# A two-layer decoder trunk: second norm row, weight low parts, forget gates, output projection and last norm rearranged together

## The chip, the cores and the metric

The kernel runs on one core of a Trainium2 chip. The metric is the time of one execution on the device, in microseconds (us), as the median of several runs. The engines are named as the profile names them: PE (TensorE, the matrix engine), DVE (VectorE), ACT (ScalarE), POOL (GpSimd) and SP (SyncE, which here only issues DMAs). Each engine works through its own list of instructions in order. An instruction whose input is not ready holds back everything behind it on that engine.

## The reference

The input is one sequence of 1024 tokens with 1024 channels, in float32. Layer 0 is a gated linear recurrence, layer 1 is forgetting attention, and a last RMSNorm follows.

```python
def lru_mixer(h, ...):
    u = h @ w_in
    xb, gate = u[..., :1536], u[..., 1536:]
    xc = causal_depthwise_conv(xb, conv_w, conv_b)
    r, i = sigmoid(block_diag(xc, wa, ba)), sigmoid(block_diag(xc, wx, bx))
    a = exp(-8.0 * r * softplus(-a_param))
    hs = associative_scan(combine, (a, sqrt(1 - a * a) * (i * xc)))
    return (hs * silu(gate)) @ w_out

def fox_mixer(h, ...):
    q, k, v, gate, f_logit = split(h @ w_in)          # 16 heads of 64
    cum = cumsum(log_sigmoid(f_logit + b_f))
    logits = q @ k.T / 8 + (cum_q - cum_k)            # causal
    o = softmax(logits) @ v
    return (o * silu(gate)) @ w_out

x = x + lru_mixer(rms_norm(x, g0), ...)
x = x + fox_mixer(rms_norm(x, g1), ...)
out = rms_norm(x, final_g)
```

## The kernel before

Every float32 product is made of three matmuls. Weights and activations are split into a high part and a low part (the rest), and `gemm_steps` (L115) multiplies high by high, weight low by high, and weight high by low, into one PSUM tile of 128x512. A weight tile is loaded (`wf`, three buffers), ACT casts its high part `wh` (`to_hi`, L85), and one engine makes the low part `wl = wf - wh` (`to_lo`, L96). That engine is `nc.gpsimd`, unless the caller names another. `wh` and `wl` have four buffers each. The sequence has two halves of 512 tokens; `c`, `h` or `half` counts them.

**Layer 0** loops over 12 blocks `n` of 128 channels: `ups` is the block's input projection, `gps` its gate's, `ops` the output projection. The first norm's factors come from `rms_row` (which calls `inv_rms`, L139): PE sums squares (`sscol`), ACT takes the root, DVE puts the inverse on the diagonal of `rs`, PE spreads it over the partitions (`rsrow`, against `onesf`), and ACT copies that back into `rs`. The norm is applied to the products afterwards: `us = ups * rs` on DVE (L271). In block 1, `ups` is two tiles, one for each half (451 and 452 in the rows below, from weights 441/442 and 447/448).

**Layer 1 begins** with `project` and `kq_units` (keys and queries of a pair of heads), then `values(0)`, which computes the values of four heads and, in 16 more columns, the forget logits `fz`. `forget(half)` transposes four `fz` tiles (`fps`), and computes the cumulated gates of that half. Constants are set on POOL and DVE on the way: `T` and `U` (rows of ones and zeros in the operands of the logits), and the causal `mask`.

**Attention** goes over 16 heads in 8 pairs. `maxima` computes blocks of logits `S`, their maxima on DVE (L673) and exponentials `p` on ACT (L678); `weigh` transposes `p` (`pt`), splits it (`ph`, `pl`) and multiplies with the values (`O`). An order string in `run` interleaves both with steps of a generator `fill`: the next pair's projections (`kq_units`, `g_units`), and after every fourth head `values(g)`, one by one without cover. At the end of a head `tr` transposes the inverse sums, two DMAs spread them over 64 partitions (`recd`, `recb`), POOL multiplies them into the gate (`scale`, L705), and `gated` multiplies the head pair's result `yo` by it on POOL (L760). Results of pairs 0 to 5 go to `y1d` in DRAM, those of the last are split where they are (`split_y`).

**From head 12 on** no more projections are left, and `fill` is the output projection: `load_y` fetches the six stored pairs of a half, `split_loaded` casts them (`yhh`, `yhl`), and `partial` multiplies them for an output block `db` and a half `c` (`ops1`). `turned(c, q)` completes quarters: it transposes the stored sum (`x1`, from `residual`) into a PSUM tile `turn`, adds the products of the last two pairs, and takes squares (ACT L867) and the weighted copy `res` (DVE L869, L872) for the last norm. Two quarters run beside head 15, two are the tail of the kernel.

The order on each engine comes from a scheduler that runs over a simulated time line. `tc.issue_after` and the order of the generators in the code bind it.

## Time and profile before

| | |
|---|---|
| median of 3 runs | 1154.62 us (1153.79 to 1159.84) |
| the profiled execution's own time | 1156.08 us |
| its span, first to last instruction | 1154.1 us |
| DVE busy | 723.0 us (63%) |
| ACT busy | 593.2 us (51%) |
| POOL busy | 230.1 us (20%) |
| low parts on POOL (L96) | 114 instructions, 166.2 us |

The span is the stretch that the trace covers; 1.98 us of the execution lie around it. Busy times are sums over the whole span. A row of a time line gives the start, the duration, the engine, the line, the operation and its tiles; what stands in square brackets is how long the engine had been idle and what it was waiting for.

### The profile page before, as it was taken

The page shows a single profiled execution, that of the slowest core. Times are in us where ns is not written, and L with a number is a line of the kernel's source. Part 1 is how long each engine was busy: PE and PEld are TensorE (multiplying, and loading weights), DVE is VectorE, ACT ScalarE, POOL GpSimd, SP SyncE. Part 2 cuts the span into 40 slices and gives each one's busy share as a digit, 9 for nine tenths or more (in the row PEclk, how much of TensorE's full clock was granted, in tenths as well). Part 3 has the DMA queues.
Part 4 walks back from the last instruction along what each step waited for, and adds up shares of the span by engine and source line. Part 5 has one row for each costly group of instructions (what it writes and reads, how often), then busy time and mean ns, then how long its engine had stood idle before and what let it go on. Part 6 is the DMA issues. An engine that isn't in the chain of part 4 may idle for free.

```text
span 1154.1 us, 15825 instructions
## 1 busy us (share of the span) xinstructions
PE 1121.8 (97%) x5713; PEld 942.8 (82%) x5713; DVE 723.0 (63%) x1222; ACT 593.2 (51%) x1081; POOL 230.1 (20%) x159
## 2 busy tenths in 40 slices
PE   9999999999999999999999999999999999979996
PEld 7788888888888887978888988889888898858874
DVE  7589766777567789566665356663666535746644
ACT  8388345355553657455555355554555534534434
POOL 1212112211121102342222122222232221011010
PEclk9999999999999999999999999999999999989999
DMA  6111111111111124353434135241352512835444
GB/s 212 51 41 51 46 56 52 41 55 41 51 55 40 56 64 157 88 134 88 120 84 107 46 88 124 79 119 45 77 129 74 129 44 67 237 104 160 130 128 182
DMA packets 63637, 105.42 MB, mean 91 GB/s; under 512 B 9444, under 2 KB 24420, under 8 KB 63560
## 3 DMA queue, kind: packets, MB, share of 16 engines
q1 hardware_dynamic: 63560, 104.42, 31.6%
q8 instruction: 45, 0.74, 0.3%
q14 instruction: 32, 0.26, 0.1%
HBM read 63.30 MB, written 15.93 MB: 69 GB/s over the span
## 4 chain that ended last, share of the span: by engine, by line
PE 86%; DVE 4%; issue 3%; DMA 3%; POOL 2%; ACT 2%; SPq 0%; POOLq 0%; ACTq 0%; DVEq 0%
PE gps L54 31%; PE ops L54 16%; PE ups L54 11%; PE vps L54 6%; PE S L54 6%; PE O L54 5%; PE pt L58 5%; PE gate L54 3%; PE turn L54 2%; DMA recb<-recd 1%; POOL sg L705 1%; POOL wl L96 1%; DMA recd<-rc 1%; DVE sq L162 1%; DVE hl L238 1%
## 5 line engine op out<-in xcount | busy, mean ns | idle before, releaser
L96 POOL TENSOR_TENSOR wl<-wf,wh 128x512 fp32r<-128x512 f32 (+1 forms) x114 | 166.2, 1463 | 664.3 <-ACT wh L85 472.2
L54 PE MATMUL gps<-hh,wh 128*128 128x512 f32 x576 | 228.9, 398 | 0.2 <-DVE qkl L565 0.2
L54 PE MATMUL gps<-hh,wl 128*128 128x512 f32 x576 | 226.7, 394 | 0.1
L54 PE MATMUL gps<-hl,wh 128*128 128x512 f32 x576 | 226.7, 393 | 0.0
L678 ACT ACTIVATE p<-S,m 128x128 f32<-128x128 f32 (+7 forms) x128 | 94.8, 741 | 141.1 <-DVE m L673 139.7
L85 ACT CAST wh<-wf 128x512 fp32r<-128x512 f32 (+2 forms) x156 | 94.4, 607 | 141.1 <-PE ops L54 41.9
L96 DVE TENSOR_TENSOR pl<-pt,ph 128x512 fp32r<-128x512 f32 (+1 forms) x198 | 98.8, 541 | 101.6 <-ACT ph L85 101.1
L54 PEld LDWEIGHTS gps<-hl,wh 128*128 128x128 f32 x576 | 108.2, 188 | 24.5
L54 PEld LDWEIGHTS gps<-hh,wl 128*128 128x128 f32 x576 | 108.7, 189 | 20.4 <-POOL wl L96 0.6
L54 PEld LDWEIGHTS gps<-hh,wh 128*128 128x128 f32 x576 | 108.5, 188 | 20.0 <-DVE qkl L565 0.4
L673 DVE CUSTOM_DVE_ANT_0 S<-S,mask 128x128 f32<-128x128 f32 (+7 forms) x128 | 97.4, 762 | 40.5 <-PE S L54 39.0
L85 ACT CAST ph<-pt 128x512 fp32r<-128x512 f32 (+1 forms) x198 | 83.0, 474 | 28.9 <-PE pt L58 23.5
L54 PE MATMUL S<-T,U 96*128 96x512 f32 (+7 forms) x384 | 92.1, 349 | 0.0
L361 DVE TENSOR_TENSOR x<-x,ops 128x512 f32<-128x512 f32 x80 | 54.1, 682 | 50.9 <-PE ops L54 50.8
L58 PE MATMUL pt<-ident,p 128*128 128x128 f32 x576 | 80.0, 275 | 0.0
L54 PEld LDWEIGHTS S<-T,U 128*128 128x128 f32 (+1 forms) x384 | 69.1, 190 | 13.2 <-ACT p L678 0.8
L54 PE MATMUL ups<-hh,wh 128*128 128x512 f32 x192 | 76.7, 400 | 2.5 <-DVE us L271 1.9
L58 PEld LDWEIGHTS pt<-ident,p 128*128 128x128 f32 x576 | 69.2, 142 | 10.7 <-issue 0.4
L54 PE MATMUL ups<-hl,wh 128*128 128x512 f32 x192 | 76.5, 398 | 0.2
L54 PE MATMUL ops<-yh,wh 128*128 128x512 f32 x192 | 76.1, 396 | 0.5 <-DVE x L453 0.5
L54 PE MATMUL vps<-wl,hh 128*128 128x256 f32 (+1 forms) x256 | 72.8, 286 | 3.7 <-POOL wl L96 3.7
L54 PE MATMUL ups<-hh,wl 128*128 128x512 f32 x192 | 76.0, 396 | 0.0
(176 smaller groups left out, 2184.3 us busy)
## 6 DMA issues: line engine op xcount, KB each, us to landing
wf<-in_w SPq DMA_DIRECT2D x100, 256.0 KB
wf<-in_wo SPq DMA_DIRECT2D x64, 128.0 KB
U<-qkh SPq DMA_DIRECT2D x64, 128.0 KB
T<-qkh SPq DMA_DIRECT2D x28, 256.0 KB
x<-in_xt SPq DMA_DIRECT2D x16, 256.0 KB
x1d<-x SPq DMA_DIRECT2D x16, 256.0 KB
wf<-in_wv SPq DMA_DIRECT2D x16, 256.0 KB
U<-qkl SPq DMA_DIRECT2D x32, 128.0 KB
```

Source lines behind the costliest of these rows:

```text
L54: pe[0] = nc.tensor.matmul(*args, **kw)
L58: pe[0] = nc.tensor.transpose(*args)
L85: nc.scalar.copy(hi, src)
L96: return eng.tensor_tensor(lo, src, f32(hi), ALU.subtract)
L162: eng.tensor_tensor(parts[0], parts[0], sq, ALU.add)
L238: nc.vector.scalar_tensor_tensor(lo, x, g_, f32(hi), ALU.mult, ALU.subtract)
L361: nc.vector.tensor_tensor(x, x, pt, ALU.add)
L673: nc.vector.tensor_tensor_reduce(S[:, :n], S[:, :n], mask[:, SEQ - n :], -1.0, -NEG, ALU.add, ALU.min, accum_out=m)
L678: seen[0] = nc.scalar.activation(p, S[:, :n], AF.Exp, bias=m, scale=-1.0, accum_out=sums[:, i : i + 1])
L705: nc.gpsimd.tensor_tensor(sg, sg, recs[hd // 2][rows, cs], ALU.mult)
```

## The change

It has eight parts, all in the order or the place of work. The arithmetic stays.

1. In block 1 of layer 0 the first half's product is issued in steps. The second four weight rows (wh 447) come after the second norm row.
2. The constants `T`, `U` and `mask` are set in the code after two steps of `values(0)`, not ahead of it.
3. `forget` becomes a generator, and its second half runs among the key and query projections.
4. `values(1)` to `values(3)` begin ahead of the last head's second run, and make low parts on DVE.
5. `kq_units` and `g_units` make low parts on DVE for pairs 1 to 7.
6. From head 12 on, the stored results are cast beside the gate projection and the first `partial`, the output blocks go two at a time, weights of the next block are split one earlier, and the last but one pair's results are split one run later.
7. The first quarter's stored sums are loaded into eight tiles of the values' pool, and the others into swapped tags.
8. In the tail, `turn` takes one-bank PSUM tiles with tag `g` or `O`, and the scaling of the first half's output becomes a side generator.

```diff
@@ layer 0
-            product(ups[0], 0, wu)
+            steps = gemm_steps(ups[0], zip(wu, raw[0]))
+            if n == 1:
+                take(steps, 2)
+                with tc.issue_after(row.ins):
+                    drain(steps)
+            drain(steps)
...
-                rms_row(sums[1], rs[:, HALF:])
+                row = rms_row(sums[1], rs[:, HALF:])[2]
@@ constants: the memsets of T and U become fixed_rows(), called below with the mask
@@ values
-                parts += split_weights(src, (2, 256 + ex), nc.scalar, nc.gpsimd)
+                parts += split_weights(src, (2, 256 + ex), nc.scalar, nc.gpsimd if ex else nc.vector)
+                if k == 2:
+                    yield
@@ kq_units, g_units
+        def low(pair):
+            return nc.vector if pair else nc.gpsimd
-                    kqw[is_k] = list(weights(w1[is_k * 8 + pair]))
+                    kqw[is_k] = list(weights(w1[is_k * 8 + pair], lo_eng=low(pair)))
-                gw[0] = list(weights(w1[16 + pair]))
+                gw[0] = list(weights(w1[16 + pair], lo_eng=low(pair)))
@@ forget
             for i in range(4):
-                transpose(pt[:HEADS, i * P : (i + 1) * P], fz[:, half * 4 + i], ident)
+                if half and i > 1:
+                    yield
+                with tc.issue_after(pe[0].ins):
+                    transpose(pt[:HEADS, i * P : (i + 1) * P], fz[:, half * 4 + i], ident)
...
         first = values(0)
-        for _ in range(9):
-            next(first)
-        forget(0)
-        drain(first)
-        forget(1)
+        next(first)
+        next(first)
+        fixed_rows()
+        mask = ...
+        take(first, 8)
+        drain(forget(0))
+        drain(first)
...
-        drain(kq_units(0, ((1, (1,)), (0, (1,)))))
+        fill = kq_units(0, ((1, (1,)), (0, (1,))))
+        gates1 = forget(1)
+        for _ in range(2):
+            next(gates1)
+            take(fill, 2)
+        drain(gates1)
+        drain(fill)
@@ gated
-            if hd >= 13:
+            if hd == 15:
                 split_y(c, pair, yo, sub)
-            else:
+            elif hd < 13:
                 nc.sync.dma_start(y1d[c, pair], yo)
@@ split_loaded: yields after every second pair
+        def beside(steps, first, more):
+            for i, _ in enumerate(steps):
+                if i >= first:
+                    next(more, None)
+                yield
+        def split_out(db):
+            if db < KT and db not in wo:
+                wo[db] = list(weights(wo1[db, :, :6], lo_eng=nc.vector))
@@ partial
-                if db not in wo:
-                    wo[db] = list(weights(wo1[db, :, :6], lo_eng=nc.vector))
+                split_out(db)
+                if c:
+                    split_out(db + 1)
@@ residual
+            if c == q == 0:
+                xs = [vpool.tile([P, 256], F32, tag=f"v{d}", name="x1", bufs=2) for d in range(KT)]
+                for d, x in enumerate(xs):
+                    nc.sync.dma_start(x, x1d[c, :, d, cs])
+                return xs
@@ turned
-                    if c == 1 and b == 1:
-                        if h == 0:
-                            two = two_banks("turn")
-                        pt = two[:, h]
-                    else:
-                        pt = ps.tile([P, HALF], F32, tag="gO"[c * q], name="turn")
+                    pt = ps.tile([P, HALF], F32, tag="gO"[c * b], name="turn")
@@ heads
-                    rest = [(db, c) for db in range(2, KT) for c in range(2)]
+                    pairs = ((0, 1), (2, 3), (4, 5), (6, 7))
+                    todo = [(db, c) for two in pairs for c in range(2) for db in two]
+                    splits = [split_loaded(c) for c in range(2)]
                     fill = chain(
                         kq_units(7),
                         g_units(7, (0,)),
                         load_y(0),
-                        g_units(7, (1,)),
+                        first_out(),
+                        beside(g_units(7, (1,)), 2, splits[0]),
                         load_y(1),
-                        split_loaded(0),
-                        partial([(0, 0), (1, 0)]),
-                        split_loaded(1),
-                        partial([(0, 1), (1, 1)] + rest),
+                        beside(beside(partial(todo), 0, splits[0]), 4, splits[1]),
...
+            if hd == 14:
+                split_y(1, 6, yos[6, 1])
             scale(hd)
             gated(hd, 0)
             side = late() if hd == 14 else iter(())
+            if hd % 4 == 3 and hd < 12:
+                vals = values(hd // 4 + 1)
+                next(vals)
             run(second, weigh(hd, 1), maxima(hd + 1, 0), fill=fill, side=side)
             drain(side)
             gated(hd, 1)
+            if hd == 13:
+                split_y(0, 6, yos[6, 0])
...
             if hd % 4 == 3 and hd < 12:
-                drain(values(hd // 4 + 1))
+                drain(vals)
```

Three places show what this does to the order of instructions. The first is on PE in layer 0, around the second norm row. The kernel before has these rows there; the next row, `ups_567`, belongs to block 2.

```order
L54 MATMUL ups_452<-hl_198,wh_447 128x512
L54 MATMUL ups_452<-hh_199,wh_447 128x512
L54 MATMUL ups_452<-hh_199,wl_448 128x512
L54 MATMUL ups_452<-hl_200,wh_447 128x512
L54 MATMUL rsrow_397<-rs_168,onesf_74 128x512 [waits DVE_49,Activation_49]
L54 MATMUL ups_567<-hh_169,wh_557 128x512 [waits DVE_49]
L54 MATMUL ups_567<-hh_169,wl_558 128x512 [waits Pool_49]
```

In the changed kernel the norm row has these neighbours.

```order
L54 MATMUL ups_452<-hh_199,wh_447 128x512
L54 MATMUL ups_452<-hh_199,wl_448 128x512
L54 MATMUL ups_452<-hl_200,wh_447 128x512
L54 MATMUL rsrow_397<-rs_168,onesf_74 128x512 [waits DVE_49,Activation_49]
L54 MATMUL ups_451<-hh_177,wh_447 128x512
L54 MATMUL ups_451<-hh_177,wl_448 128x512
L54 MATMUL ups_451<-hl_178,wh_447 128x512
L54 MATMUL ups_451<-hh_179,wh_447 128x512
```

Between the sums of squares and the norm row stood 24 `ups` matmuls, and now 12 stand there. The other 12, of `ups_451` with weight 447, have moved behind it, ahead of `ups_567`.

The second place is POOL at the beginning of layer 1, where the fourth low part of the values' weights and the constants stand. Before, the order is this.

```order
L96 TENSOR_TENSOR wl_3719<-wf_3715,wh_3718 128x544 [waits DMAHW7_49,DMAHW6_49,Activation_49]
L477 MEMSET mask_3593 128x1024 [waits DMAHW4_49,DMAHW2_49,DMAHW5_49,DVE_49,Activation_49]
L489 MEMSET T0_3598 64x1024 [waits Pool_49]
L489 MEMSET T1_3599 64x1024
L96 TENSOR_TENSOR wl_3726<-wf_3722,wh_3725 128x544 [waits DMAHW0_49,DMAHW1_49,Activation_49,Pool_49]
L478 AFFINE_SELECT mask_3593<-mask_3593 128x1024
```

In the changed kernel it is this.

```order
L96 TENSOR_TENSOR wl_3706<-wf_3702,wh_3705 128x544 [waits DMAHW7_49,DMAHW6_49,Activation_49]
L490 MEMSET T0_3593 64x1024 [waits DMAHW2_49,DMAHW4_49,DVE_49,DMAHW5_49,Activation_49,Pool_49]
L490 MEMSET T1_3594 64x1024
L642 MEMSET mask_3731 128x1024 [waits Pool_49]
L96 TENSOR_TENSOR wl_3713<-wf_3709,wh_3712 128x544 [waits DMAHW1_49,DMAHW0_49,Activation_49]
L643 AFFINE_SELECT mask_3731<-mask_3731 128x1024 [waits Pool_49]
```

The three memsets have changed places among themselves; the fourth low part still stands behind all three.

The third place is ACT in head 14, around the cast of the first result of pair 6 (`yhh` from `yo_8855`, which POOL has to finish first). Before, the order is this; the rows from `yhl` cast the stored results of the second half.

```order
L678 ACTIVATE p_9473,sums_9430<-S_9468,m_9471 128x256 [waits DVE_49]
L85 CAST yhh_9426<-yo_8855 128x512 [waits Pool_49]
L85 CAST yhh_9299<-yhl_9300 128x512 [waits DMAHW0_49]
L85 CAST yhh_9302<-yhl_9303 128x512 [waits DMAHW1_49]
L85 CAST yhh_9305<-yhl_9306 128x512 [waits DMAHW2_49]
L85 CAST yhh_9308<-yhl_9309 128x512 [waits DMAHW3_49]
L85 CAST yhh_9311<-yhl_9312 128x512 [waits DMAHW5_49]
L85 CAST yhh_9314<-yhl_9315 128x512 [waits DMAHW6_49]
L85 CAST ph_9507<-pt_9498 128x512 [waits PE_49,Activation_49]
```

In the changed kernel that cast has other neighbours.

```order
L696 ACTIVATE p_9477,sums_9426<-S_9472,m_9475 128x256 [waits DVE_49]
L85 CAST ph_9503<-pt_9494 128x512 [waits PE_49,Activation_49]
L85 CAST ph_9506<-pt_9494 128x512 [waits PE_49]
L85 CAST wh_9538<-wf_9536 128x512 [waits DMAHW7_49,PE_49]
L85 CAST wh_9544<-wf_9542 128x256 [waits DMAHW7_49,PE_49]
L85 CAST yhh_9636<-yo_8855 128x512 [waits Pool_49]
L696 ACTIVATE p_9532,sums_9426<-S_9527,m_9530 128x384 [waits DVE_49]
L85 CAST ph_9565<-pt_9557 128x512 [waits PE_49,Activation_49]
```

The six casts of stored results have left this place (they stand earlier in the list). The cast that needs POOL now stands behind two casts of transposed exponentials and two of output weights, and ahead of the exponential of the third logit block.

More of the change, by code (lines that the diff above doesn't have):

```diff
@@ L473, in trunk @@
         at = l1.enter_context(pool("at", 2))
-        mask = tu.tile([P, SEQ], BF16, name="mask")
-        nc.gpsimd.memset(mask, 0.0)
-        nc.gpsimd.affine_select(
-            out=mask, in_=mask, pattern=[[-1, SEQ]], compare_op=ALU.is_ge, fill=NEG, base=SEQ - P, channel_multiplier=1
-        )
         T = [tu.tile([P, 2, SEQ], F32R, tag=f"T{s}", name=f"T{s}") for s in range(2)]
@@ L626, in trunk @@
         first = values(0)
-        for _ in range(9):
-            next(first)
-        forget(0)
+        next(first)
+        next(first)
+        fixed_rows()
+        mask = tu.tile([P, SEQ], BF16, name="mask")
+        nc.gpsimd.memset(mask, 0.0)
+        nc.gpsimd.affine_select(
+            out=mask, in_=mask, pattern=[[-1, SEQ]], compare_op=ALU.is_ge, fill=NEG, base=SEQ - P, channel_multiplier=1
+        )
+        take(first, 8)
+        drain(forget(0))
         drain(first)
-        forget(1)
         gw = [None]
@@ L826, in residual @@
         def residual(c, q):
[L827 removed]
+            cs = slice(q * 256, (q + 1) * 256)
+            if c == q == 0:
[3 more added lines that the diff above has]
+                return xs
+            xs = [wpool.tile([P, 2, 256], F32, tag=("wl", "wh")[q], name="x1") for d in range(4)]
             for d, x in enumerate(xs):
[L829 to L830 removed]
+                nc.sync.dma_start(x, x1d[c, :, 2 * d : 2 * d + 2, cs])
+            return [x[:, i] for x in xs for i in range(2)]
         def turned(c, q):
@@ L968, in trunk, with finish @@
             left[1, q] = residual(1, q)
-        r = root_mean(ssq[0])
-        for i, o in enumerate(first_half):
-            nc.vector.tensor_scalar(o, o, r[:, i : i + 1], None, ALU.mult)
-            nc.sync.dma_start(out[i], o)
-        run("." * 18, fill=chain(turned(1, 0), turned(1, 1)))
+        def finish():
+            r = root_mean(ssq[0])
+            yield
+            for i, o in enumerate(first_half):
+                nc.vector.tensor_scalar(o, o, r[:, i : i + 1], None, ALU.mult)
+                nc.sync.dma_start(out[i], o)
+                yield
+                yield
+        run("." * 18, fill=chain(turned(1, 0), turned(1, 1)), side=finish())
 def layout(inputs):
```

20 lines of the change are left out of this document (11 added, 9 removed).

## The prediction

> **What bounds the kernel now.** I read the page first: the span, the busy times and the chain that ended last.
>
> ```profile
> span 1154.1 us, 15825 instructions
> PE 1121.8 (97%) x5713; PEld 942.8 (82%) x5713; DVE 723.0 (63%) x1222; ACT 593.2 (51%) x1081; POOL 230.1 (20%) x159
> PE 86%; DVE 4%; issue 3%; DMA 3%; POOL 2%; ACT 2%; SPq 0%; POOLq 0%; ACTq 0%; DVEq 0%
> ```
>
> PE is busy for 97% of the span and makes up 86% of the chain. The change takes no matmul away, so all that it can win is idle time of PE and time that PE spends at a lower clock. The second view is therefore the list of PE's waits (line, who is waited for: us in total, times, longest).
>
> ```profile
> PE ops L54 <- ACT yhh L85: 8.9, 1, 8.9
> PE turn L54 <- DVE res L869: 4.6, 2, 2.7
> PE vps L54 <- POOL wl L96: 3.7, 4, 1.1
> PE ups L54 <- DVE us L271: 1.9, 1, 1.9
> PE turn L54 <- DMA x<-x1d: 1.9, 1, 1.9
> PE fps L58 <- DVE fz L535: 1.4, 1, 1.4
> PE vps L54 <- ACT wh L85: 1.0, 3, 0.3
> ```
>
> Together 23.4 us. The third view cuts the time into stretches; the last three numbers of a row are the granted clock, the DMA share and GB/s.
>
> ```profile
> 49.60:53.02 3.42, 3.42 (x10) 2.67 (x9) 2.19 (x3) 2.74 (x3) 0.48 (x1) 0.50 0.26 81
> 1018.49:1022.40 3.91, 3.91 (x12) 3.11 (x13) 3.76 (x7) 2.54 (x5) 0.00 (x0) 0.50 0.00 0
> 1111.15:1114.56 3.41, 3.41 (x14) 2.71 (x13) 0.76 (x2) 1.15 (x4) 0.00 (x0) 0.50 0.00 0
> 1136.57:1140.00 3.43, 3.43 (x19) 2.87 (x20) 1.01 (x4) 1.71 (x4) 0.00 (x0) 1.00 1.01 394
> ```
>
> Three waits (of 1.9, 8.9 and 1.9 us) are followed by a stretch in which PE is fully busy at half clock. The work of such a stretch would take half of it, so it costs 3.42/2 = 1.7, 3.91/2 = 1.95 and 3.41/2 = 1.7 us more. The wait of 2.7 us that ends at 1136.57 is followed by a full clock. So a wait of some 2 us can cost 1.7 us more, and need not.
>
> The Trainium skill, "TensorE: Matmul & The Clock Gate", section "HAM oscillation — how this bites in real kernels", gives as the rule that PE must have no idle gap above about 3.4 us. By that rule the two gaps of 1.9 us would not halve the clock; this trace differs, with half clock in 3.42 and 3.41 us behind them.
>
> **The change part by part.** *Second norm row.* The rows are two of PE, then ACT, and two of DVE.
>
> ```profile
> 45.85 1.02 PE L54 MATMUL rsrow<-rs,onesf 128*128 128x512 f32 x2
> 48.81 0.50 PE L54 MATMUL ups<-hh,wh 128*128 128x512 f32 x1 [1.94 <-DVE us L271]
> ...
> 46.91 0.58 ACT L152 COPY rs<-rsrow 128x512 f32<-128x512 f32 x1 [2.92 <-PE rsrow L54]
> ...
> 40.95 0.88 DVE L149 TENSOR_SCALAR rs<-ident,rms 128x128 f32<-128x128 f32 x4
> 47.53 1.23 DVE L271 TENSOR_TENSOR us<-ups,rs 128x1024 f32<-128x1024 f32 x1 [5.70 <-ACT rs L152]
> ```
>
> The diagonal is ready at 40.95 + 0.88 = 41.83, but the row waits behind 24 matmuls until 45.85. By the order it stands behind 12. Twelve such matmuls take 2.79 us:
>
> ```profile
> 1023.76 2.79 PE ops L54 x12
> ```
>
> So the row starts at 45.85 - 2.79 = 43.06 (behind 41.83, so it does not wait), and everything behind it comes 2.79 us earlier: the copy at 44.12, `us` at 44.74 to 45.97. PE meanwhile does the 12 moved matmuls and wants `ups_567` when it would have in any case, after 45.85 + 1.02 = 46.87, a little less as matmuls overlap. The 1.94 us go, and with them the half clock: 1.94 + 1.7 = **3.6 us**. What hides the rest is the 12 matmuls; the margin is 0.9 us. Without that cover up to 1 us would stay.
>
> *Constants.* On POOL, before:
>
> ```profile
> 468.07 0.95 POOL L477 MEMSET mask<- 128x1024 bf16 x1 [2.75 <-issue]
> 469.08 1.84 POOL L489 MEMSET T<- 64x1024 f32 x2
> 471.00 1.33 POOL L96 TENSOR_TENSOR wl<-wf,wh 128x544 fp32r<-128x544 f32 x1
> ```
>
> The fourth low part comes 2.9 us after the memsets begin, and PE waits 1.1 us for it (the longest of the four waits for `wl` in the list above). The order rows show it still behind three memsets with the same semaphores. This part does not do what its words say: **0**, at best the 1.1 us, at worst 0.2 us more.
>
> *Forget gates.* The third `fps` stands 12 matmuls later than before, which is 2.79 us, and its wait was 1.4 us: **1.4 us** go, with projections as cover.
>
> *Values 1 to 3.* Of the first (at 639 us), and the low part on DVE elsewhere (34 of the same size, 23.2 us, 685 ns each):
>
> ```profile
> 639.89 1.28 POOL L96 TENSOR_TENSOR wl<-wf,wh 128x512 fp32r<-128x512 f32 x1 [6.30 <-ACT wh L85]
> 641.23 0.39 PE L54 MATMUL vps<-wl,hh 128*128 128x256 f32 x1 [0.86 <-POOL wl L96]
> ...
> L96 DVE TENSOR_TENSOR wl<-wf,wh 128x512 fp32r<-128x512 f32 x34 | 23.2, 685 | 7.5 <-ACT wh L85 7.5
> ```
>
> The cast still waits for a buffer that the last projection frees, so the 1.0 us for ACT stay. The low part shrinks from 1.28 to 0.69, three times: 3 x 0.59 = **1.8 us**; between 0 (DVE busy just then) and 3 x 0.86 = 2.6 (the early loads help too). `next(vals)` puts the first two weight loads ahead of the head's last loads in SP's list; nothing there is late now.
>
> *Low parts of keys, queries and gates.* Forty-two go from POOL to DVE, with the 12 of the values 54: 54 x 0.685 = 37 us more on DVE. Two pairs take 143 us:
>
> ```profile
> 640.00:783.00 143.00, 141.79 (x822) 123.89 (x822) 78.58 (x172) 72.39 (x165) 35.29 (x25) 1.00 0.35 90
> ```
>
> DVE has 78.6 us of work there and gets 16 x 0.685 = 11.0 more: 63%. PE waits for no low part of a projection in this trace. I take **0**: nothing to win, and a loss is the last rival.
>
> *Head 14.* The chain behind the wait of 8.9 us:
>
> ```profile
> 1004.87 0.27 PE L689 MATMUL tr<-ident,sums 128*8 128x128 f32 x1
> ...
> 1006.98 2.37 DMA recd<-rc
> 1009.37 4.08 DMA recb<-recd
> ...
> 1013.59 2.34 POOL L705 TENSOR_TENSOR sg<-sg,recb 64x1024 f32<-64x1024 f32 x1 [38.42 <-DMA recb<-recd]
> 1016.00 1.26 POOL L760 TENSOR_TENSOR yo<-yo,sg 128x512 f32<-128x512 f32 x1
> 1017.30 0.62 ACT L85 CAST yhh<-yo 128x512 fp32r<-128x512 f32 x1 [6.18 <-POOL yo L760]
> 1018.49 0.79 PE L54 MATMUL ops<-yhh,wh 128*128 128x512 f32 x1 [8.85 <-ACT yhh L85]
> ```
>
> ACT's cast of `yo` waits for POOL, and behind it stood the six casts that PE wanted. By the order these are done earlier, so PE goes on at 1009.3. But the new order brings a new wait: the cast stands ahead of the exponential `p_9532`, which frees the PSUM tile that PE needs for the fourth logit block. In PE's list `tr` now stands behind the eight transposes and eleven `ops1` matmuls, some 4.1 us later, at 1008.9. The chain from there: copy and issue 0.6, `recd` 2.37, `recb` 4.08, POOL 0.1 + 2.34 + 0.1 + 1.26, so `yo` is done at 1019.9, its cast at 1020.5, `p_9532` (0.6 as an estimate, from neighbours of 0.47 and 1.12) at 1021.1. PE has 42 products and 15 transposes from `tr` to that block, about 9.9 us by the pitch above and 0.1 us for a transpose, and gets there at 1018.8. It waits **2.3 us** in place of 8.85. Behind that ACT cast are held the exponential, two casts of `pt` and the next output weights; DVE's maximum and PE wait for these. The bounds are 0 (a faster `recb`, more work ahead) and 3.5 (DVE or ACT late by a cast each). Half clock may follow: two of the three rows with waits of about 2 us say so, so I count 1.7 in. The part wins 8.85 + 1.95 - 2.3 - 1.7 = **6.8 us**, between 4 and 10.8.
>
> *First quarter's loads.*
>
> ```profile
> 1105.98 4.44 DMA x<-x1d
> ```
>
> The last load lands at 1110.42, because its buffer is one that the output weights free late. The new tiles are in the values' pool; by SP's order the last of eight stands right behind the last `recb`, at about 1101, and with 4.44 us lands at 1105.5, ahead of the 1108 at which PE needs it. The 1.9 us and the half clock behind go: 1.9 + 1.7 = **3.6 us**, at least 1.9.
>
> *Tail.*
>
> ```profile
> 1131.91 2.74 DVE L971 TENSOR_SCALAR res<-res,ssq 128x1024 f32<-128x1024 f32 x4
> ...
> 1136.57 0.66 PE L54 MATMUL turn<-ident,x 128*128 128x128 f32 x4 [2.66 <-DVE res L869]
> ...
> 1146.14 0.66 PE L54 MATMUL turn<-ident,x 128*128 128x128 f32 x4 [1.93 <-DVE res L869]
> ```
>
> A two-bank tile is free only when both halves have been read, and DVE is held by four scalings. With four one-bank tiles PE can go two tiles further. DVE's list still has the scalings together, but PE needs its tile 3.7 us later than now. Both waits go: **4.6 us**, at least 3.
>
> New small waits are likely where casts, splits and output blocks change places (layer 0's later blocks, 985 to 1100): I set 1 us against it, 0 to 3.
>
> **Sum:** 3.6 + 0 + 1.4 + 1.8 + 0 + 6.8 + 3.6 + 4.6 - 1 = 20.8 us. The profiled execution took 1156.08 (span 1154.1 and 1.98 around it), which gives 1135.3; it lay 1.46 above the median of 1154.62, which gives 1133.8. I say 1134.
>
> **The rivals.** *All waits go,* the fourth low part's and head 14's too: 20.8 + 1 + 1.1 + 4.0 = 26.9, so 1127.7 to 1129.2. For it speaks the scheduler's freedom; against it the order rows at both places.
>
> *Waits move instead of going.* The POOL chain in head 14 is not shorter, and every engine's list is new there. With 4 us won in head 14, half clock left at the other two places (3.4), 3 us of new waits and 1.6 less in the tail: 20.8 - 2.8 - 3.4 - 2 - 1.6 = 11, so 1143.6 to 1145. By the skill's rule on gaps named above the two stretches of half clock would have other causes than the gaps and stay, which alone would give 1137.4; against it speaks that no such stretch lies between 53 and 1009 us, where PE has no gap of 1.9 us.
>
> *Slower: DVE's list as the new bound.* POOL's waits held up nobody. On DVE a low part that waits for a cast or a weight load holds back the maximum behind it, then ACT's exponential, and PE's transposes. The price is 54 times the delay that reaches PE. At 0.39 us each the 20.8 us are gone, and at 0.6 us the kernel is 11.6 us slower (1166). Against it: DVE has 37% of its time free and PE has other work between a logit block and its transposes. One effect goes the other way:
>
> ```profile
> 453.35 0.68 DVE L162 TENSOR_TENSOR sq<-sq 128x512 f32<-128x512 f32 x1
> 454.62 1.79 DVE L162 TENSOR_TENSOR sq<-sq 128x512 f32<-128x512 f32 x1
> ```
>
> The same DVE operation takes 0.68 us alone and 1.79 us beside a low part on POOL. The Trainium skill, "GPSIMD Engine Reference", section 1 "Specifications", says that POOL shares its SBUF interfaces with VectorE, with contention for DVE instructions that have two SBUF inputs; the two rows agree.
>
> **How the numbers follow.** The forecast's own cases (1130 to 1140) get 0.64, "all waits go" 0.12, "waits move" 0.14, a DVE delay of about 0.3 us (near 1150) 0.06, a larger one 0.04. The range from 1126 to 1146 takes in the bounds of all terms (best: 3.6 + 1.1 + 1.4 + 2.6 + 10.8 + 3.6 + 4.6 = 27.7, which is 1126.9 from the median) and leaves out the last two cases. A measurement tells about 0.5% from no change, which is 5.8 us: faster means below 1148.8. Faster 0.88, same 0.08, slower 0.04.
>
> **What would show it.** In the profile after: no wait of `ups` for `us`, and full clock from 46 to 56 us; the wait for POOL's `wl` once, near 471 us; none for `fz`; values waiting for a DVE `wl` for some 0.3 us, three times; one wait of PE's `S` for ACT's `p` near 1005 us, of about 2 us; none for `x1`, none for `res`. DVE busy near 760 us, POOL near 150. The forecast is wrong if PE's busy time grows at full clock, if PE waits in the attention for `p`, `pl` or `wl`, or if one of the removed waits stands there with another name.

## The result, and the profile after

| | before | after |
|---|---|---|
| median of 4 runs | 1154.49 us (1153.79 to 1159.84) | 1139.92 us (1138.22 to 1140.99) |
| profiled execution | 1156.08 us, span 1154.1 | 1139.88 us, span 1138.1 |

The ratio is 0.9862, with a 95% interval of 0.9831 to 0.9894. The changed kernel is faster, by 14.6 us in the medians and by 16.0 us in the spans. The forecast was 1134.0, in a range of 1126 to 1146.

From the page of the changed kernel: the span, the busy times, and the chain that ended last.

```profile
span 1138.1 us, 15824 instructions
PE 1118.1 (98%) x5713; PEld 937.9 (82%) x5713; DVE 760.2 (67%) x1276; ACT 592.2 (52%) x1081; POOL 162.2 (14%) x105
PE 85%; DVE 7%; ACT 3%; DMA 3%; issue 2%; POOL 1%; SPq 0%; ACTq 0%; DVEq 0%; POOLq 0%
```

DVE got the 37 us of low parts that were counted for it, and POOL lost 68. In the chain DVE's share went from 4% to 7%, ACT's from 2% to 3%, POOL's from 2% to 1%, and PE's from 86% to 85%. The list of PE's waits in the changed kernel shows what PE waits for now (us in total, times, longest).

```profile
PE vps L54 <- DVE sg L662: 2.1, 3, 0.7
PE S L54 <- ACT p L696: 2.0, 2, 1.5
PE gate L54 <- ACT th L296: 1.6, 1, 1.6
PE gps L54 <- DVE qkl L571: 1.3, 1, 1.3
PE gps L54 <- DVE sg L307: 1.2, 1, 1.2
...
PE ups L54 <- ACT wh L85: 0.9, 1, 0.9
PE vps L54 <- ACT wh L85: 0.9, 3, 0.3
PE vps L54 <- DVE wl L96: 0.7, 3, 0.2
PE gps L54 <- POOL wl L96: 0.6, 1, 0.6
```

Of the seven kinds of wait that the prediction listed, six are gone; the values' wait for ACT is left (1.0, now 0.9). The values' wait for POOL's `wl` (2.6 us at the first weights of values 1 to 3) is gone under that name only: 0.7 us for DVE's `wl` stand in its place. And rows stand here that were not there before: `sg` twice, `th`, two for weights in layer 0; the wait for `qkl` has grown from 0.2 to 1.3 us. To see where the time went, I divide both executions at the starts of six matmuls of PE: the first `ups`, the last `ops` of layer 0, the first logit block `S`, the first `ops1`, the first `turn`, the last `O`; the last boundary is the start of PE's last matmul. The stretches before (length, then PE's busy time, the other engines, and clock, DMA share and GB/s at the end):

```profile
5.92:460.46 454.54, 451.46 (x1957) 364.78 (x1958) 338.31 (x399) 255.71 (x324) 82.65 (x50) 1.00 0.20 65
460.46:511.68 51.22, 48.64 (x308) 43.62 (x307) 29.68 (x59) 24.07 (x43) 21.13 (x17) 1.00 0.39 106
511.68:997.09 485.41, 481.64 (x2741) 418.22 (x2740) 270.80 (x590) 245.92 (x557) 112.96 (x77) 1.00 0.37 96
997.09:1105.57 108.48, 99.63 (x495) 82.98 (x495) 61.83 (x128) 43.91 (x99) 11.16 (x7) 0.95 0.47 139
1105.57:1124.43 18.86, 16.82 (x95) 13.91 (x94) 7.88 (x16) 6.73 (x21) 0.72 (x1) 0.91 0.39 124
1124.43:1147.80 23.37, 18.78 (x103) 15.00 (x102) 12.27 (x27) 11.74 (x30) 0.73 (x1) 1.00 0.55 203
```

The same stretches after:

```profile
6.09:462.13 456.04, 450.56 (x1957) 363.39 (x1958) 341.55 (x400) 256.13 (x324) 83.72 (x51) 1.00 0.20 65
462.13:510.72 48.59, 48.59 (x309) 43.60 (x308) 28.81 (x59) 23.99 (x42) 17.80 (x15) 1.00 0.42 114
510.72:998.53 487.81, 482.84 (x2742) 417.31 (x2740) 305.82 (x643) 246.06 (x559) 46.90 (x25) 1.00 0.36 96
998.53:1098.71 100.18, 97.95 (x495) 81.32 (x495) 61.84 (x128) 42.70 (x98) 11.62 (x7) 1.00 0.53 161
1098.71:1113.52 14.81, 14.81 (x96) 12.79 (x94) 7.80 (x16) 6.72 (x21) 0.75 (x1) 1.00 0.28 87
1113.52:1131.85 18.33, 18.33 (x103) 15.15 (x102) 11.77 (x27) 11.45 (x30) 0.73 (x1) 1.00 0.65 236
```

| stretch | what the change does there | forecast | measured |
|---|---|---|---|
| layer 0 | norm row | -3.6 | **+1.50** |
| to the first `S` | constants, forget gates | -1.4 | -2.63 |
| to the first `ops1` | values, low parts on DVE | -1.8 | **+2.40** |
| to the first `turn` | head 14, and 1 us set against it | -5.8 | -8.30 |
| to the last `O` | first quarter's loads | -3.6 | -4.05 |
| to the last matmul | tail | -4.6 | -5.04 |

The start-up took 0.17 us more and the end 0.06 less, so the sum is 16.0 where 20.8 was forecast. The last three stretches won 2.5 + 0.5 + 0.4 us more than forecast, and the one to the first `S` 1.2 more. Layer 0 and the stretch with the values and the low parts lost where they should have won; they fell 5.1 and 4.2 us short.

### The profile page after: what moved, and what is told of

The parts are those of the page before. It is cut to its first block, busy times and chain, and to the rows that moved or that the text cites. A ratio compares the mean times of both kernels' runs of the same rounds, so it can differ in the third digit from the quotient of the medians.

```text
span 1138.1 us, 15824 instructions
## 1 busy us (share of the span) xinstructions
PE 1118.1 (98%) x5713; PEld 937.9 (82%) x5713; DVE 760.2 (67%) x1276; ACT 592.2 (52%) x1081; POOL 162.2 (14%) x105
## 4 chain that ended last, share of the span: by engine, by line
PE 85%; DVE 7%; ACT 3%; DMA 3%; issue 2%; POOL 1%; SPq 0%; ACTq 0%; DVEq 0%; POOLq 0%
PE gps L54 31%; PE ops L54 15%; PE ups L54 9%; PE vps L54 7%; PE S L54 6%; PE O L54 6%; PE pt L58 5%; PE turn L54 3%; PE gate L54 2%; DVE xc L275 1%; PE sscol L54 1%; ACT wh L85 1%; DMA wf<-in_wo 1%; DVE a L328 0%; DMA wf<-in_w 0%
## 5 line engine op out<-in xcount | busy, mean ns | idle before, releaser
L96 POOL TENSOR_TENSOR wl<-wf,wh 128x512 fp32r<-128x512 f32 (+1 forms) x60 | 97.3, 1627 | 398.6 <-ACT wh L85 342.6
L723 POOL TENSOR_TENSOR sg<-sg,recb 64x1024 f32<-64x1024 f32 (+1 forms) x17 | 39.1, 2298 | 462.7 <-DMA recb<-recd 462.7
L96 DVE TENSOR_TENSOR wl<-wf,wh 128x512 fp32r<-128x512 f32 x96 | 69.8, 732 | 25.7 <-ACT wh L85 24.8
L54 PE MATMUL vps<-wh,hh 128*128 128x256 f32 (+1 forms) x256 | 73.7, 288 | 3.0 <-DVE sg L662 2.1
```

Source lines behind the costliest of these rows:

```text
L54: pe[0] = nc.tensor.matmul(*args, **kw)
L96: return eng.tensor_tensor(lo, src, f32(hi), ALU.subtract)
L723: nc.gpsimd.tensor_tensor(sg, sg, recs[hd // 2][rows, cs], ALU.mult)
```

## The experiments

Medians of the kernel before were 1154.5 to 1156.3 us on the chips used, so kernels are compared by their ratio to it. Edits are against the changed kernel unless said otherwise. In the expectations the stretch from the first `S` to the first `ops1` is written as 585.4, 587.8 and 585.5 us; it is 485.4, 487.8 and 485.5, and the differences between them hold.

### Layer 0: what the norm row did

The wait for `us` and the half clock behind it are gone: PE has no idle time in 40 to 60 us of the changed kernel. But between 85 and 109 us it has four new waits. On ACT of the kernel before, block 1 (time line: start, duration, engine, line, operation):

```profile
69.30 1.04 ACT L85 CAST xch<-xc 128x1024 fp32r<-128x1024 f32 x1
70.24 0.69 ACT L296 ACTIVATE ti<-gate,hbx 128x512 f32<-128x512 f32 x1
70.94 1.28 ACT L326 ACT_TABLE_LOAD   x1
```

The same place on ACT of the changed kernel:

```profile
67.09 1.04 ACT L85 CAST xch<-xc 128x1024 fp32r<-128x1024 f32 x1
68.15 1.28 ACT L326 ACT_TABLE_LOAD   x1
69.44 1.06 ACT L326 ACTIVATE m<-m 128x1024 f32<-128x1024 f32 x1
70.52 1.28 ACT L296 ACT_TABLE_LOAD   x1
71.82 0.69 ACT L296 ACTIVATE ti<-gate,hbx 128x512 f32<-128x512 f32 x1
```

The scheduler has put the square root (L326) ahead of the second half's gate `ti` (L296). The root and two loads of ACT's tables, 3.6 us together, now stand ahead of `ti`. It comes 1.6 us later than before, although the cast ahead of it is 2.2 us earlier. On DVE of the changed kernel:

```profile
72.53 1.23 DVE L325 SCALAR_TENSOR_TENSOR ti<-ti,xc 128x1024 f32<-128x1024 f32 x1 [3.04 <-ACT ti L296]
```

DVE stands idle for 3.04 us and then has no free time until about 110 us, where PE, 3.7 us ahead of before (349 matmuls by 81.3 us; before, 350 by 85.0), runs into it. Three kernels test this. **u_row** takes the norm row's move back out of the change; **row_alone** puts it alone into the kernel before.

```diff
-            steps = gemm_steps(ups[0], zip(wu, raw[0]))
-            if n == 1:
-                take(steps, 2)
-                with tc.issue_after(row.ins):
-                    drain(steps)
-            drain(steps)
+            product(ups[0], 0, wu)
```

> The change without its edit of the second norm row. Theory A: that edit reorders ACT and PE in the next blocks of layer 0 and makes DVE's work there late; the four new waits between 85 and 110 us (5.0 us) are its own, so it costs 1.7 us by the end of layer 0 rather than winning 3.6. Then these four waits are gone, the wait for us (1.9) and the half clock behind it are back, layer 0 ends 1.7 us earlier, and 1.2 us of that are lost again near 471 us, where PE then comes ahead of the fourth low part once more: about 1139.5, no change that can be told from 1139.9. Theory B: the edit wins its 3.6 us and the waits belong to other edits: about 1143.5.

> The kernel before with the edit of the second norm row alone. Theory A: the wait for us is gone, four waits of together about 5 us stand between 85 and 110 us, layer 0 ends 1.7 us later, the wait near 471 us shrinks by 1.2: about 1155 (from 1154.5). Theory B: 1150.9.

Measured: `u_row` 1137.54 us (1136.69 to 1138.24), ratio 0.9841 (0.9825 to 0.9858). `row_alone` 1158.60 (10 runs) against 1156.23 (13 runs), ratio 1.0027 (1.0014 to 1.0041). In `u_row` PE waits 1.9 us for `us` again and has no wait between 80 and 112 us. From PE's list of waits in `row_alone`:

```profile
PE gate L54 <- ACT th L296: 1.6, 1, 1.6
...
PE gps L54 <- DVE sg L307: 1.2, 1, 1.2
...
PE ups L54 <- ACT wh L85: 0.8, 1, 0.8
PE gps L54 <- POOL wl L96: 0.6, 1, 0.6
```

The kernel before has none of these four between 80 and 112 us. They come with this edit and go with it. Layer 0 takes 453.90 us without it and 456.04 with it in the changed kernel, 454.54 and 456.02 in the kernel before. The last `ops` of layer 0 starts at 461.7 to 463.0 us in the eight profiled kernels that have this edit as it stands, and at 460.1 to 460.6 in the three without it. So the edit wins its 3.6 us and loses 5.1 to 5.7; the four waits add up to 4.3 of that, and where the rest went is not shown. Alone it makes the kernel slower, by 0.27%. `u_row` was expected at 1139.5, because 1.2 us were to be lost again in a wait for the fourth low part near 471 us; that wait did not come.

**pin_sqrt** keeps the edit and binds the square root behind the gate's second half.

```diff
-                nc.scalar.activation(t_, t_, AF.Sqrt, scale=1.0 / 16.0)
+                with tc.issue_after(s["last"].ins):
+                    nc.scalar.activation(t_, t_, AF.Sqrt, scale=1.0 / 16.0)
```

> The change with one pin more: in recur, the square root (and its table load) of a block is issued after the last tanh of the block's gates. Theory A1: the late DVE chain of block 1 comes from ACT, which takes the square root and two table loads ahead of the second half's tanh (71.82 us), so DVE idles 3.0 us ahead of ti near 72 us. Then that idle time falls below 1 us, the waits between 85 and 110 us fall from 5.0 to about 2.5, layer 0 ends some 2.5 us earlier, 1.2 of it is lost again near 471 us: about 1138.5. Theory A2: DVE is full there in any order, and an earlier PE only waits longer: the waits stay at 5.0, 1139.9.

Measured: 1138.49 us (1136.46 to 1139.42), ratio 0.9845 (0.9831 to 0.9860). On DVE of `pin_sqrt` the same instruction now has no idle time ahead of it:

```profile
69.32 1.22 DVE L325 SCALAR_TENSOR_TENSOR ti<-ti,xc 128x1024 f32<-128x1024 f32 x1
```

Layer 0 takes 453.24 us, 2.8 less than in the change. Two of the four waits are left (`th` 1.6, `wh` 0.9). So the square root's place is about half of the loss. The total fell less, since this profile has a stretch of half clock at 641 us (below).

**less_dve** was to show whether DVE's load is the rest: it leaves out one multiplication on DVE (L305) in blocks 0 to 3.

```diff
-            state[n] = dict(xc=xc, x=(xh, xl), w=(wgh, wgl), tap=tap)
+            state[n] = dict(xc=xc, x=(xh, xl), w=(wgh, wgl), tap=tap, scale=n > 3)
...
-                nc.vector.tensor_tensor(g_, g_, rs[:, cs], ALU.mult)
+                if s.get("scale", True):
+                    nc.vector.tensor_tensor(g_, g_, rs[:, cs], ALU.mult)
```

> The change without the multiplication of the gate products by the norm in blocks 0 to 3 of layer 0 (left out: four DVE instructions of 1.22 us). Theory A1: ACT's order (square root ahead of the last tanh) makes the waits between 85 and 110 us: they stay above 4 of 5.0 us. Theory A2: DVE's load is the bound there: the waits fall to 2.5 us or less, and layer 0 ends at least 2.5 us earlier.

Measured: 1143.82 us in a single run. The scheduler planned the blocks anew, and a wait of 2.5 us for a low part on POOL, with half clock behind it, stands in place of the four. It tells nothing about DVE's load; that the rest is DVE's load stays argued, not shown.

### Constants

**u_const** is `u_row` with the constants back at their old place.

```diff
+        mask = ...
         T = [tu.tile([P, 2, SEQ], F32R, tag=f"T{s}", name=f"T{s}") for s in range(2)]
...
+        fixed_rows()
...
-        fixed_rows()
-        mask = ...
         take(first, 8)
```

> The change without its edit of the second norm row (as in the first run) and with the constants at their old place in the code. Without the first, layer 0 ends as early as before, and PE reaches the fourth low part as early. Theory K: the edit of the constants changes nothing, and that PE did not wait there in the changed kernel is due to the late layer 0 and to how early the last store of x lands: a wait like that of the first run (0). Theory L: with the old place the first memset waits longer, and PE waits 1.1 us for the fourth low part as before; then this edit won 1.1 us, and this kernel takes 1.1 us more than the first run's 1137.5.

Measured: 1138.18 us (1136.76 to 1139.47), ratio 0.9848 (0.9826 to 0.9869), against 0.9841 of `u_row`. On POOL of `u_const` the memsets stand ahead of the fourth low part again:

```profile
466.76 0.95 POOL L478 MEMSET mask<- 128x1024 bf16 x1 [1.60 <-ACT wh L85]
...
469.70 1.36 POOL L96 TENSOR_TENSOR wl<-wf,wh 128x544 fp32r<-128x544 f32 x1
```

PE waits for none of it, with the constants at either place. The edit is worth nothing, as forecast. The 1.1 us of the kernel before went with something else. Near the end of layer 0 a `sq` on DVE starts 0.6 us behind a low part on POOL. These are the rows of that `sq` in the changed kernel and in `tail_two` (below), which has the same layer 0 and the same constants:

```profile
456.30 0.68 DVE L162 TENSOR_TENSOR sq<-sq 128x512 f32<-128x512 f32 x1
...
456.58 1.78 DVE L162 TENSOR_TENSOR sq<-sq 128x512 f32<-128x512 f32 x1
```

POOL's low part takes 2.42 us in the first and 1.81 in the second: one of the two instructions is held up. Where it is DVE's (the kernel before, `row_alone`, `pin_sqrt`, `tail_two`), the last store of `x` is issued 3.5 us after the start of the last `ops`, and PE waits 0.4 to 1.1 us for the fourth low part, behind POOL's memsets. In the other ten profiled kernels it is POOL's, the store is issued 2.7 to 2.8 us after it, and PE does not wait. So the wait goes with the outcome of this meeting and not with the constants; no run varied the meeting by itself.

### Forget gates

**u_forget** computes the second half in one piece ahead of the projections, as before.

```diff
-        fill = kq_units(0, ((1, (1,)), (0, (1,))))
-        gates1 = forget(1)
-        for _ in range(2):
-            next(gates1)
-            take(fill, 2)
-        drain(gates1)
-        drain(fill)
+        drain(forget(1))
+        drain(kq_units(0, ((1, (1,)), (0, (1,)))))
```

> The change with forget(1) issued in one piece ahead of the projections again. Theory G: the edit only moves the wait: PE waits 1.4 us for fz again, and the new wait of 1.3 us for DVE's qkl near 511 us shrinks to 0.2: 1140.2, no change. Theory H: the edit won its 1.4 us: 1141.3.

Measured: 1142.11 us (1139.46 to 1143.02), ratio 0.9879 (0.9863 to 0.9896). In its trace the wait is back (`fps` for `fz`, 1.4 us), but another has gone. DVE of the changed kernel, just ahead of the wait of 1.3 us for `qkl`:

```profile
508.00 1.27 DVE L624 TENSOR_TENSOR_SCAN cum<-unit,cum,z 16x512 f32<-16x512 f32 x1
...
511.32 0.67 DVE L96 TENSOR_TENSOR cp<-cum,cp 16x512 fp32r<-16x512 f32 x1
511.92 0.67 DVE L571 SCALAR_TENSOR_TENSOR qkl<-gps,qkh 128x512 fp32r<-128x512 f32 x1
```

The forget gates' own work on DVE (`cum`, `cp`) now stands between the keys' parts, and PE waits for these. From the end of layer 0 to the first `vps` of values 1 it is 169.14 us in the change and 168.97 in `u_forget`: in the profiled executions the wait has moved, and nothing is won. The medians lie 2.2 us apart, with ranges that overlap, and that of `u_forget` is nearer to what was expected if the edit had won its 1.4 us. Its profiled execution is its fastest (1139.46 us, granted clock 0.999); the three others took 1142.0 to 1143.0 us at 0.995 to 0.997, while all four of the change were granted 0.999. Half clock behind the wait for `fz` would fit. No trace of these three shows it, so whether the edit won those 2 us stays open.

### Values, and the low parts on DVE

**values_pool** and **kqg_pool** give the 12 low parts of the values, and the 42 of keys, queries and gates, back to POOL.

```diff
-                parts += split_weights(src, (2, 256 + ex), nc.scalar, nc.gpsimd if ex else nc.vector)
+                parts += split_weights(src, (2, 256 + ex), nc.scalar, nc.gpsimd)
```

```diff
-            return nc.vector if pair else nc.gpsimd
+            return nc.gpsimd
```

> The change with the low parts of the later values' weights (12 instructions) back on POOL. Theory C: on DVE they stand ahead of the gate's last product, whose PSUM tile PE needs 0.7 us later, so what POOL's slower subtraction cost comes back as a wait for sg; on POOL three waits for wl (about 0.9 each) stand in place of three for sg (0.7) and three for DVE's wl (0.2): within 0.5 us of 1139.9. Theory D: moving them won the 1.8 us that I forecast: 1141.7.

> The change with the low parts of the key, query and gate weights (42 instructions) back on POOL. From the first logit matmul to the first ops1 matmul the kernel before took 585.4 us, the change 587.8. Theory E: these 42 on DVE hold back maxima here and there and cost about 0.8 of the 2.4 us: 587.0, total 1139. Theory F: they cost nothing, the 2.4 us are the wait for qkl near 511 us and the values: 587.8, total 1139.9.

Measured: `values_pool` 1139.95 us (1138.82 to 1141.12), ratio 0.9860 (0.9846 to 0.9875); `kqg_pool` 1140.18 (1139.50 to 1141.78), 0.9862 (0.9847 to 0.9877). Both are as fast as the change. In `values_pool` these waits of PE stand in place of the change's `sg` and `wl`:

```profile
PE vps L54 <- POOL wl L96: 2.5, 3, 0.9
```

2.1 + 0.7 us for DVE, or 2.5 for POOL: the shorter low part won nothing. The reason stands on DVE of the changed kernel, at the first such place.

```profile
640.36 0.69 DVE L96 TENSOR_TENSOR wl<-wf,wh 128x512 fp32r<-128x512 f32 x1
...
641.81 0.69 DVE L662 SCALAR_TENSOR_TENSOR sg<-sg,gps 128x512 f32<-128x512 f32 x1
```

And on PE:

```profile
641.11 0.39 PE L54 MATMUL vps<-wl,hh 128*128 128x256 f32 x1 [0.22 <-DVE wl L96]
...
642.55 0.39 PE L54 MATMUL vps<-wh,hh 128*128 128x256 f32 x1 [0.70 <-DVE sg L662]
```

The low part is early, but it stands ahead of `sg`. `sg` is the last reader of the gate projection's PSUM tile, and the second block of values needs that tile. If the tile is the limit, another tile must free more than the low part. **values_bank** gives the second block of each later group a tile that stands idle there, that of the logits.

```diff
-                if ex and st % 2:
+                if (ex and st % 2) or st == 1:
                     pt = ps.tile([P, SEQ], F32, tag="S", name="vps")[:, : 256 + ex]
```

> The change with the second block of each later group of values put into a PSUM tile of the logits' tag S instead of g. Theory C: the wait of 0.7 us for sg, three times, is a wait for the g tile that the gate's last product still holds; in another bank it goes, and the low parts on DVE keep what they win over POOL: from the first logit matmul to the first ops1 matmul 587.8 falls to about 585.5, total 1137.5. Rival: the next head's logits and transposes then wait for the S tiles: 587.8, total 1139.9.

Measured: 1133.20 us (1132.55 to 1135.27), ratio 0.9809 (0.9780 to 0.9838). The stretch from the first `S` to the first `ops1`:

```profile
510.80:992.36 481.56, 480.85 (x2741) 417.00 (x2740) 306.09 (x642) 246.28 (x559) 47.15 (x25) 1.00 0.36 97
```

That is 6.3 us less than in the change. PE has no wait left between 600 and 990 us, not even for ACT: with two free tiles the scheduler has 18 matmuls of the second block to put ahead of the fourth weight. The list had 3.7 us of waits there, the wait for `qkl` ahead of 600 us is 0.6 us shorter in this execution, and PE's busy time in the stretch fell by 2.0 us; what made that last part is not shown. It was expected at 1137.5.

### Head 14, and the tail

ACT, POOL and PE of the changed kernel in head 14:

```profile
1019.81 1.35 POOL L778 TENSOR_TENSOR yo<-yo,sg 128x512 f32<-128x512 f32 x1
...
1021.19 0.62 ACT L85 CAST yhh<-yo 128x512 fp32r<-128x512 f32 x1 [3.25 <-POOL yo L778]
1021.72 0.57 ACT L696 ACTIVATE p<-S,m 128x384 f32<-128x384 f32 x1
...
1022.43 0.74 PE L54 MATMUL S<-T,U 128*128 128x512 f32 x2 [1.50 <-ACT p L696]
```

This is the chain that was forecast, step by step, and near the 1021 us of its working (the list of signs said 1005). **pin_split** binds the cast behind the last exponential issued ahead of it, so that the exponential need not wait for POOL.

```diff
-                split_y(0, 6, yos[6, 0])
+                with tc.issue_after(seen[0].ins):
+                    split_y(0, 6, yos[6, 0])
```

> The change with the cast of pair 6's first result pinned behind the last exponential issued before it. If the wait of 1.5 us of PE's S for ACT's p near 1022 us is due to that cast standing ahead of the exponential, it goes: 1138.4. If POOL's chain is waited for elsewhere as well, a wait of the same size comes later in the stretch: 1139.9.

Measured: 1138.66 us (1137.46 to 1139.14), ratio 0.9845 (0.9830 to 0.9860). PE has no wait between 990 and 1100 us, and the stretch to the first `turn` is 97.85 us in place of 100.18.

**tail_two** puts back the old two-bank tile in the tail, and no more.

```diff
-                    pt = ps.tile([P, HALF], F32, tag="gO"[c * b], name="turn")
+                    if c == 1 and b == 1:
+                        if h == 0:
+                            two = two_banks("turn")
+                        pt = two[:, h]
+                    else:
+                        pt = ps.tile([P, HALF], F32, tag="gO"[c * q], name="turn")
```

> The change with the old PSUM tiles of the tail (two banks for the second block of a quarter). If the tiles alone made PE wait for res, two waits of together 4.6 us are back and the stretch from the last O matmul to the last matmul takes 23.0 us instead of 18.3: 1144.6. If the scaling as a side generator did it: 18.3, 1139.9.

Measured: 1147.60 us in a single run. The row of the kernel before is back in PE's list:

```profile
PE turn L54 <- DVE res L911: 4.6, 2, 2.7
```

The last stretch takes 24.91 us in place of 18.33; 1.7 of it is a stretch of half clock. So the gain needs the tiles: without them the side generator for the scaling wins nothing. Whether the tiles win it without the generator was not run. Nor does a run take out the early casts of head 14, or the eight tiles of the first quarter's loads: that these made their gains rests on their waits, 8.9 and 1.9 us in the list before and not in the list after.

### The parts that won, with the losses mended

**best** joins `pin_sqrt`, `kqg_pool`, `values_bank` and `pin_split`, and binds the constants behind the fourth low part.

```diff
-        fixed_rows()
+        with tc.issue_after(low_part[0].ins):
+            fixed_rows()
...
-        nc.gpsimd.memset(mask, 0.0)
+        with tc.issue_after(low_part[0].ins):
+            nc.gpsimd.memset(mask, 0.0)
```

> The change with all mends together: the square root pinned behind the last tanh, the constants pinned behind the fourth low part, the low parts of keys, queries and gates back on POOL, the second block of values in an S tile, the cast of pair 6's first result pinned behind the exponential. If the mends add up (2.8 in layer 0 less 0.7 at the constants, 0.7 for the pinned constants, 1.3, 2.3 and 1.5): 1132. If they only move waits to the next engine: above 1136.

Measured: 1129.49 us (1127.98 to 1132.13), ratio 0.9776 (0.9749 to 0.9802). It beats both kernels. It was expected at 1132, with 2.3 us for the tile, which alone had won 5.75 (next section). From the page of `best`:

```profile
PE 1114.8 (99%) x5713; PEld 939.1 (83%) x5713; DVE 734.5 (65%) x1234; ACT 591.2 (52%) x1079; POOL 217.0 (19%) x147
```

Left are the waits for `th` in layer 0 (1.6 us), for `qkl` (1.2), some others, and a stretch of half clock at 107 us.

## Why the prediction was right, and which steps failed

**Range, sign and bound were right.** PE stayed the bound, and what could be won was its idle time and half clock. The sum was 4.8 us too large, by two steps that failed and one that was undone a little later. That the total came so near is partly luck: two stretches fell 9.3 us short, and the others won 4.6 more than forecast, 1.1 of it by a wait that was put at 0 and went for a reason outside that edit. And one of the prediction's own signs of being wrong came true, "if one of the removed waits stands there with another name": at values 1 to 3, 2.6 us for POOL's `wl` became 2.8 for `sg` and DVE's `wl`.

**Second norm row (3.6 us).** "The 1.94 us go, and with them the half clock" came true. What failed is the sum's last term, "new small waits are likely", set at 1 us for layer 0's later blocks and for head 14 together. In layer 0 alone the loss is 3.6 + 1.5 = 5.1 us. The move changed ACT's order in the same block, and that was not in the working. `row_alone` and `u_row` show the loss on both sides, and `pin_sqrt` shows about half of it to be the square root's place.

**Values 1 to 3 (1.8 us).** "The low part shrinks from 1.28 to 0.69, three times" is right as a duration and wrong as a gain. The prediction followed the weight and not the PSUM tile that the next block needs. `values_pool` shows that the low part's engine is worth nothing, `values_bank` that the tile is worth 5.75 us: from the first `vps` of values 1 to the first `ops1` it takes 361.51 us, and the change 367.26.

**Forget gates (1.4 us).** The wait for `fz` went, and the one for `qkl` behind it grew from 0.2 to 1.3 us; from the first `S` to the first `vps` of values 1 the change takes 120.55 us, the kernel before 119.03. The prediction said that projections cover the transposes; it did not look at who waits behind the gates' work on DVE. That is the rival "waits move instead of going", at a place that it did not name. What the edit is worth in the medians stays open (above).

**Low parts of keys, queries and gates (0).** In total `kqg_pool` is no faster than the change. From values 1 to the first `ops1` the change takes 367.26 us, the kernel before 366.38, `values_pool` (only these 42 on DVE) 366.89, and `kqg_pool` 368.22 with 1.7 us of half clock in it, so about 366.5. By these single executions the 42 low parts cost 0.5 to 0.8 us on DVE, 0.01 to 0.02 us each; that is an estimate, and the medians do not show it. The slower rival needed 0.39 us for each, some twenty times that.

**Constants (0)** held for the edit: the fourth low part stayed behind the memsets, and nothing came of their new order. The sign "the wait for POOL's `wl` once, near 471 us" did not come, for the reason given above.

**Head 14 (6.8 us)** was right in its mechanism, and two sizes in it were too careful: the new wait took 1.5 us in place of 2.3, and no half clock followed it (1.7). That is 2.5 us more, which is what the stretch shows. One sum in its working is off: 42 products at 2.79/12 us and 15 transposes at 0.1 are 11.3 us, not 9.9, and by 11.3 the wait would have been 0.9. PE took 10.2 us from `tr` (1010.75) to the block (1020.93). The 1 us for other small waits was used up here.

**First quarter's loads (3.6) and tail (4.6)** came out at 4.05 and 5.04. The first includes the half clock that went with its wait.

## What to carry to other kernels

When an edit moves work on one engine, look at the order of the other engines in the same stretch for what the scheduler has swapped: here a square root and two table loads ahead of a tanh were about half of a loss that was larger than the edit's gain. Before an operation is made shorter because somebody waits for it, ask what the waiting engine needs next; here it was a PSUM tile, and a second free tile won three times what the shorter operation was meant to.

## What was not expected of the hardware

**Half clock without a long gap.** In `pin_sqrt` PE waits 0.7 us at the first values, as in the change, and is then at half clock for 3.41 us (the granted clock is the number behind POOL's):

```profile
640.77:644.18 3.41, 3.41 (x19) 3.41 (x18) 0.26 (x1) 0.00 (x0) 0.00 (x0) 0.50 0.20 77
```

The changed kernel, same code, at the same place behind the same waits:

```profile
643.00:646.41 3.41, 3.41 (x31) 3.41 (x30) 0.65 (x2) 0.53 (x2) 0.13 (x1) 1.00 0.22 84
```

`kqg_pool` and `pin_split` have the stretch there too, and the 1.5 us wait in head 14 of the change had none. So gaps that add up to under 2 us cost 1.7 us more in one execution and nothing in another, which is the size of several of the edits studied here. It also bears on the medians: the four executions of the change were all granted 0.999, those of `kqg_pool` 0.997 to 0.998, and `pin_split` took 1137.5 us at 1.0 and 1138.3 to 1139.1 at 0.997. In the kernel before, the three stretches of half clock end at 53.02, 1022.40 and 1114.56 us; between these lie 969.38 and 92.16 us, which are 284 and 27 times 3.4133 us, so the ends fall on one grid. The Trainium skill, "TensorE: Matmul & The Clock Gate", section "Part 1: The HAM clock gate", describes an activity window of 3413 ns that runs on freely; the length of 3.41 us agrees with it, and a dependence on where in the window a gap falls would fit, though no run here varied that alone.

**DVE beside POOL.** The scan of block 1 took 2.29 us on DVE of the kernel before, while POOL was idle. In the change, where a low part of 1.29 us began on POOL at 77.69, it took 1.1 us more:

```profile
77.74 3.39 DVE L328 TENSOR_TENSOR_SCAN a<-a,ti 128x1024 f32<-128x1024 f32 x1
```

The loser is not always DVE. In the meeting of `sq` and a low part near the end of layer 0, POOL starts 0.6 us ahead in every kernel; in four executions DVE then took 1.1 us longer (1.79 in place of 0.68), in ten POOL took 0.6 longer (2.42 in place of 1.82).
